# State space stage: TensorE's work pinned to an order written out by hand

## The chip, the cores and the metric

One core of one Trainium2 chip runs the whole program. The time is the device time of one execution in microseconds (us); of three executions of the kernel before, the median is 1193.76 us (1191.71 to 1194.17). TensorE (PE in the profile) does matrix products and transposes, VectorE (DVE) and ScalarE (ACT) work elementwise, SyncE's queue (SP) issues the DMAs.

## The reference, cut to what matters

Two layers act on 256 latent tokens and 256 context tokens of width 1024. Layer 0 is attention and a feed-forward part; layer 1 is a state space mixer, whose context stream only supplies the states, and a feed-forward part on the latent stream. The change lies in the state space mixer:

```python
z, xbc, dt = jnp.split(u @ w_in, [SSM_D_INNER, SSM_D_INNER + SSM_CONV_DIM], axis=-1)
xbc = jax.nn.silu(depthwise_conv(xbc, conv_w, conv_b))
xs, bm, cm = jnp.split(xbc, ...)                      # x: 32 heads of 64; B and C: 4 groups of 128
dt = jax.nn.softplus(dt + dt_bias)                    # two directions x 32 heads
# per direction: a = dt * a_neg, a_cs = cumsum(a)
states = einsum(B, exp(a_cs[-1] - a_cs), x * dt)      # of the context
y_diag = einsum((C B^T) * exp(segsum(a)), x * dt)     # latent, inside the sequence
y_off  = einsum(C, states, exp(a_cs))                 # latent, from the context's states
y = (y_f + y_b + x * d_skip) * silu(z)
y = y * rsqrt(mean(square(y)) + eps) * norm_g         # mean over each of 4 groups of 512 channels
y_lat = y @ w_out
```

## The kernel before, in words

All projections run on weights that come as 1 MB blocks (`raw`) through SP's queue; each 128-wide weight tile is split into a high part (`wh`, ScalarE, L61) and a low part (`wl`, VectorE, L62), and a product (`gemm`, L75) is 24 matmuls: eight k steps of high times high, high times low, low times high. Up to two tiles are split ahead (`next_w`); four split tiles and two `raw` blocks have room.

The state space stage (`layer1`, L976) works on channels times tokens, in four groups of 512 channels. It takes, in the program's order:

- six `z` products (256 columns, L825), then `dt_chain` (L770): the product `dt` (its own weight block `wdt`, split at L777 and L778), some 25 VectorE instructions (L787 to L817, among them a reciprocal and a scan) with three ScalarE exponentials, two small DMAs to `dq` in DRAM, and four transposes (L821, L822) whose result `sT` holds per-token factors.
- `ssm_in(g)` for each group g: products B (512 columns) and C (256), four x tiles (512 columns: latent and context) and, from group 1 on, the rest of the z tiles (two in group 1, four in groups 2 and 3). Each of B, C and x goes through `conv` (L747): ScalarE reads the bank, four VectorE instructions (L758) add the taps, ScalarE takes tanh, one or two VectorE instructions (L763) give the result. Each x tile is then transposed to tokens (L868, L869: four transposes) and scaled by `sT` into `xt` (ScalarE, eight instructions, L875) and `xw` (VectorE, L878). After x tile 0 come the products of C and B (`cb`, L885) and B's transposes (`bt`, L894). Last come the context's states `S` (L905).
- `ssd(g)` for each group: for each of four tiles, A and E are loaded from `dq` (L924, L925), ScalarE and VectorE make the masked factors W and the scaled C in E (L931 to L935), TensorE makes y (L947: 12 products of fp32, 24 matmul records, on half the array's columns, 128x64), VectorE finishes y (L949, L951), ScalarE squares it, and TensorE sums the squares (`rms`, L954, on a quarter of the columns, 128x32). Then `rstd` (L206) makes the group's root: a copy, two small products (`t`), square root and reciprocal, two products that spread it (`b`), and y is normalised and split (L963 to L965).

`weave` (L968) alternates a step of `ssd(g-1)` with a step of `ssm_in(g)`; after group 3 it alternates `ssd(3)` with the output products `so`. That is only the order in which the program is traced. A planner then lays out each engine's instructions: it goes through all of them in time, by its own estimates of durations, and gives each engine the earliest-traced instruction that is ready; so a ready product overtakes a transpose that waits. On the chip each engine goes through its list in order. PSUM has eight banks: four `mm` (products), three `aux` (transposes, `cb`, y, S, the root, and `rms` over a whole `ssd`), one `md`.

Of the kernel before, what the change touches and what calls it, by code (L numbers as in the profile page):

```python
# [8 lines left out]
F32 = mybir.dt.float32  # L9
# [27 lines left out]
NZ = 6  # L37


class Net:  # L40
# [23 lines left out]
    def next_w(self, ahead=2, whole=False):  # L64
# [8 lines left out]
        return wh.rearrange("p (k c) -> p k c", c=128), wl.rearrange("p (k c) -> p k c", c=128)  # L73

    def gemm(self, ps, w, ah, al, c0, c1, ks=range(8)):  # L75
        mm = self.nc.tensor.matmul
# [86 lines left out]
    def run(self, gen):  # L163
        for _ in gen:
            pass

# [38 lines left out]

    def rstd(self, ps, nm, scale, eps):  # L206
# [12 lines left out]
        for i in range(2):  # L219
            c = slice(128 * i, 128 * i + 128)  # L220
            nc.vector.tensor_scalar(d[:, c], self.ident, r[:, i:i + 1], 32.0 * 1024, op0=ALU.mult, op1=ALU.mult)
            nc.tensor.matmul(b[:, c], self.avg, d[:, c], start=True, stop=True)
        return b[:, :256]

    def ln_joint(self, s, nm, mps, X):
        nc = self.nc
        mu = self.spread(mps, nm + "m")
        vps = self.bank("aux", f"{nm}v")
        for q in range(4):
            xs = X[:, 2 * q:2 * q + 2, :]  # L230
            nc.vector.tensor_tensor(xs, xs, mu.unsqueeze(1).broadcast_to([128, 2, 256]), op=ALU.subtract)
            sq = self.t2.tile([128, 2, 256], F32, tag="t2", name=f"{nm}q")
            nc.scalar.activation(sq, xs, AF.Square)
            self.colsum(vps, sq, range(2 * q, 2 * q + 2))
        return self.rstd(vps, nm + "w", 1.0, self.eps)

# [533 lines left out]
    def dt_chain(self, uh, ul):  # L770
        nc, tc = self.nc, self.tc
        mm = nc.tensor.matmul
# [7 lines left out]
        ps = self.bank("mm", "dt")[:64, :]  # L780
# [36 lines left out]
        st(R[64:128], R[64:128], 0.125, dt[64:128], op0=ALU.mult, op1=ALU.mult)  # L817
        pt = self.bank("aux", "dtt", (128, 384))
        for i in range(2):
            c = slice(128 * i, 128 * i + 128)  # L820
            nc.tensor.transpose(pt[:, 192 * i:192 * i + 128], R[:, c], self.ident)  # L821
            nc.tensor.transpose(pt[:, 192 * i + 128:192 * i + 192], dt[0:64, c], self.ident[:64, :64])  # L822
        nc.scalar.copy(self.sT, pt.rearrange("p (i h) -> p i h", i=2))

# [11 lines left out]
    def ssm_in(self, g, uh, ul):  # L836

        nc = self.nc
        mm = nc.tensor.matmul
        sp = self.sp  # L840
# [16 lines left out]
        Bt = sp.tile([128, 2, 128], F32, tag="Bt", name=f"Bt{g}")  # L857
        for j in range(4):
            w = self.next_w()
            ps = self.bank("mm", f"x{g}{j}")  # L860
            self.gemm(ps, w, uh, ul, 0, 512)
            xl = self.xl()
            xc = sp.tile([128, 256], F32, tag="xc", name=f"xc{g}{j}")
            G["xl"].append(xl)
            self.conv(ps, 4 * g + j, 2, [xl, xc])
            pt = self.bank("aux", f"xt{g}{j}")
            for i in range(2):
                nc.tensor.transpose(pt[:, 128 * i:128 * i + 128], xl[:, 128 * i:128 * i + 128], self.ident)  # L868
                nc.tensor.transpose(pt[:, 256 + 128 * i:384 + 128 * i], xc[:, 128 * i:128 * i + 128], self.ident)  # L869
            for d in range(2):  # L870
                o = 128 + 32 * d + 8 * g + 2 * j
                for i in range(2):
# [8 lines left out]
                    self.sT[:, :, o:o + 2].unsqueeze(3).broadcast_to([128, 2, 2, 64]), op=ALU.mult)  # L881
            if j == 0:
                pb = self.bank("aux", f"cb{g}")
                for i in range(2):
                    mm(pb[:, 256 * i:256 * i + 256], B[:, 128 * i:128 * i + 128], C, start=True, stop=True)  # L885
                cf = G["cb0"] = sp.tile([128, 384], F32, tag="cf", name=f"cf{g}")
                cb = G["cb1"] = sp.tile([128, 384], F32, tag="cb", name=f"cb{g}")
                nc.vector.tensor_mul(cf[:, 0:256], pb[:, 0:256], self.tri[:, 0:256])
                nc.vector.tensor_mul(cf[:, 256:384], pb[:, 384:512], self.tri[:, 0:128])
                nc.vector.tensor_mul(cb[:, 0:128], pb[:, 0:128], self.tri[:, 256:384])  # L890
                nc.vector.tensor_mul(cb[:, 128:384], pb[:, 256:512], self.tri[:, 128:384])
                pb = self.bank("aux", f"bt{g}", (128, 256))
                for i in range(2):
                    nc.tensor.transpose(pb[:, 128 * i:128 * i + 128], B[:, 256 + 128 * i:384 + 128 * i], self.ident)  # L894
                nc.scalar.copy(Bt, pb.rearrange("p (i n) -> p i n", i=2))
            yield
        if g:
            for j in range(max(4 * g, NZ), 4 * g + 4):
                self.z_tile(j, uh, ul)
                yield  # L900
        G["S"] = []
# [9 lines left out]
    def ssd(self, g, yh, yl):  # L911
        nc = self.nc
        sp = self.sp
        mm = nc.tensor.matmul
        G = self.G[g]
        ys = []
        rps = self.bank("aux", f"rms{g}")
        for j in range(4):
            M, Cs = [], []
            for d in range(2):  # L920
# [16 lines left out]
                Cs.append(E)  # L937
            yield
            ps = self.bank("aux", f"y{g}{j}")[:, :256]
# [13 lines left out]
            nc.scalar.activation(sq, y, AF.Square)  # L953
            mm(rps[32 * j:32 * j + 32, :256], self.ones, sq, start=True, stop=True)  # L954
            ys.append(y)
            yield

        rs = self.rstd(rps, f"rms{g}", 2.0, self.eps4)
        for j in range(4):
# [16 lines left out]
    def layer1(self):  # L976
# [12 lines left out]
        with tc.tile_pool(name="dq", bufs=1, space=DRAM) as dqp:  # L989
            dq = dqp.tile([2, 64, 256], F32, name="dq")  # L990
            self.dq = dq
            with tc.tile_pool(name="sp", bufs=2) as sp:
                self.sp = _Multi(tc, sp, dict(cy=2, ct=1, B=1, C=2, xt0=2, xt1=2, xw0=1, xw1=1, Bt=1, xc=1,
                                              cf=2, cb=2, S0=1, S1=1, A=2, E=2, W=2))
                for j in range(NZ):
                    self.z_tile(j, uh, ul)
                self.dt_chain(uh, ul)
                self.run(self.ssm_in(0, uh, ul))
                for g in range(1, 4):
                    self.weave(self.ssd(g - 1, yh, yl), self.ssm_in(g, uh, ul))  # L1000
                acc = [[self.bank("mm", f"so{i}{h}") for h in range(2)] for i in range(2)]
# [172 lines left out]
```

## Time and profile before

| | |
|---|---|
| median of three executions | 1193.76 us |
| the profiled execution | 1194.7 us |
| its span, first to last instruction | 1192.9 us |
| PE busy | 1140.3 us, 96% |
| DVE busy | 839.5 us, 70% |
| ACT busy | 604.3 us, 51% |
| mean granted TensorE clock | 0.984 of full |

A matmul's duration in the profile contains filling and draining that overlap its neighbours, so the distance from one start to the next is what it costs. The state space stage runs from about 660 us (first z product) to about 978 us (`so`, with the last group's root inside).

### The profile page before, as it was taken

What the parts mean: (1) busy time and instruction counts of PE and PEld (TensorE: products, weight loads), DVE (VectorE), ACT (ScalarE), POOL (GpSimd) and SP (SyncE); (2) the same over time, 40 slices, a digit from 0 to 9 for tenths busy, and PEclk for the clock granted to TensorE, in tenths of its full rate; (3) what the DMA queues carried; (4) which work ended last, traced back from release to release, by engine and by line L of the source; (5) the groups of instructions that cost most, each with busy time, mean ns of one, the idle gap of its engine ahead of it and who ended that gap; (6) DMA issues with size and microseconds to landing.
All of it is one profiled execution on the core that took longest, in us unless ns stands there. A gap on an engine that the chain in (4) does not pass through costs nothing.

```text
span 1192.9 us, 18539 instructions
## 1 busy us (share of the span) xinstructions
PE 1140.3 (96%) x6976; PEld 917.5 (77%) x6976; DVE 839.5 (70%) x1701; ACT 604.3 (51%) x1382; POOL 48.1 (4%) x79
## 2 busy tenths in 40 slices
PE   5999999998999999999999999999999996999996
PEld 4766666887987878887898777777777575898895
DVE  4498677677967677763434879889898769565566
ACT  4376566325532322321422737687868857454551
POOL 1200000003100000000000310000000000000000
PEclk8999999999999999999999989999999998999999
DMA  8834322342445466762222124443545572555551
GB/s 323 305 106 156 128 85 94 91 157 72 159 160 182 157 226 207 249 215 92 85 71 87 64 107 128 131 153 129 189 142 155 186 242 83 200 177 182 202 181 71
DMA packets 41433, 182.79 MB, mean 153 GB/s; under 512 B 4608, under 2 KB 5248, under 8 KB 28288
## 3 DMA queue, kind: packets, MB, share of 16 engines
q1 hardware_dynamic: 41056, 181.36, 45.1%
q8 instruction: 55, 0.90, 0.3%
q10 hardware_dynamic: 288, 0.26, 0.1%
q14 instruction: 34, 0.28, 0.1%
HBM read 180.41 MB, written 1.18 MB: 152 GB/s over the span
## 4 chain that ended last, share of the span: by engine, by line
PE 79%; DVE 8%; DMA 5%; ACT 5%; issue 1%; DVEq 0%; SPq 0%; ACTq 0%
PE f0a L79 5%; PE f0a L80 5%; PE f0a L81 5%; PE f0b L79 5%; PE f0b L81 5%; PE f0b L80 5%; PE y L947 3%; PE o L508 2%; PE f L265 2%; PE f L264 2%; PE f L263 2%; PE f1a L81 2%; PE f1a L79 2%; PE f1a L80 2%; DMA raw<-in_wall 2%; PE x L81 2%
## 5 line engine op out<-in xcount | busy, mean ns | idle before, releaser
L61 ACT CAST wh<-raw 128x512 fp32r<-128x512 f32 x404 | 237.6, 619 | 400.5 <-PE f0b L80 126.3
L62 DVE TENSOR_TENSOR wl<-raw,wh 128x512 fp32r<-128x512 f32 x404 | 268.4, 686 | 129.3 <-ACT wh L61 128.4
L79 PE MATMUL f0b<-f0fh,wh 128*128 128x512 f32 (+1 forms) x320 | 113.8, 356 | 0.0
L79 PE MATMUL f0a<-u1h,wh 128*128 128x512 f32 (+1 forms) x320 | 112.2, 353 | 1.5 <-ACT u1h L183 1.5
L81 PE MATMUL f0b<-f0fh,wl 128*128 128x512 f32 (+1 forms) x320 | 111.9, 350 | 0.0
L80 PE MATMUL f0a<-u1l,wh 128*128 128x512 f32 (+1 forms) x320 | 111.4, 350 | 0.0
L81 PE MATMUL f0a<-u1h,wl 128*128 128x512 f32 (+1 forms) x320 | 111.4, 349 | 0.0
L80 PE MATMUL f0b<-f0fl,wh 128*128 128x512 f32 (+1 forms) x320 | 111.1, 347 | 0.1
L142 DVE SCALAR_TENSOR_TENSOR ma<-wm,cs,ma 128x1024 f32<-128x1024 f32 x70 | 88.7, 1280 | 17.8 <-DMA wm<-in_w_mod 17.7
L79 PEld LDWEIGHTS f0a<-u1h,wh 128*128 128x128 f32 x320 | 61.1, 192 | 11.8 <-ACT u1h L183 2.3
L81 PEld LDWEIGHTS f0b<-f0fh,wl 128*128 128x128 f32 x320 | 60.1, 188 | 10.4 <-issue 2.1
L79 PEld LDWEIGHTS f0b<-f0fh,wh 128*128 128x128 f32 x320 | 60.1, 188 | 10.4 <-issue 2.6
L80 PEld LDWEIGHTS f0b<-f0fl,wh 128*128 128x128 f32 x320 | 60.2, 188 | 9.7 <-issue 1.4
L81 PEld LDWEIGHTS f0a<-u1h,wl 128*128 128x128 f32 x320 | 61.2, 191 | 8.0 <-issue 0.4
L80 PEld LDWEIGHTS f0a<-u1l,wh 128*128 128x128 f32 x320 | 61.0, 191 | 7.7 <-issue 0.4
L79 PE MATMUL f1a<-u4h,wh 128*128 128x256 f32 x224 | 63.5, 284 | 0.0
L81 PE MATMUL f1a<-u4h,wl 128*128 128x256 f32 x224 | 63.5, 283 | 0.0
L80 PE MATMUL f1a<-u4l,wh 128*128 128x256 f32 x224 | 63.4, 283 | 0.0
L79 PE MATMUL x<-u2h,wh 128*128 128x512 f32 x128 | 51.5, 402 | 2.2 <-DVE cy L758 2.2
L931 ACT ACTIVATE W<-A,sT 128x128 f32<-128x128 f32 (+1 forms) x128 | 50.0, 458 | 3.8 <-PE y L947 2.5
L351 DVE SCALAR_TENSOR_TENSOR X<-f0b,mT,X 128x256 f32<-128x256 f32 x48 | 21.0, 478 | 44.0 <-PE f0b L81 44.0
L81 PE MATMUL x<-u2h,wl 128*128 128x512 f32 x128 | 51.3, 402 | 0.3 <-DVE wl L62 0.3
(439 smaller groups left out, 2747.3 us busy)
## 6 DMA issues: line engine op xcount, KB each, us to landing
raw<-in_wall SPq DMA_DIRECT2D x102, 1024.0 KB, 5.0
wm<-in_w_mod SPq DMA_DIRECT2D x96, 512.0 KB, 4.3
A<-dq SPq DMA_DIRECT2D x32, 256.0 KB, 4.7
E<-dq SPq DMA_DIRECT2D x32, 256.0 KB, 5.0
X<-in_xT SPq DMA_DIRECT2D x8, 256.0 KB, 8.1
gate<-in_rows SPq DMA_DIRECT2D x2, 512.0 KB, 12.9
out_dram<-Xt SPq DMA_DIRECT2D x4, 256.0 KB, 2.0
mixg<-in_rows SPq DMA_DIRECT2D x1, 512.0 KB, 6.1
```

The source lines that it names most:

```text
L61: nc.scalar.copy(h, src[:, c])
L62: nc.vector.tensor_sub(l, src[:, c], h.bitcast(F32))
L79: mm(ps, wh[:, k, :], ah[k][:, c0:c1], start=(k == 0), stop=False)
L80: mm(ps, wh[:, k, :], al[k][:, c0:c1], start=False, stop=False)
L81: mm(ps, wl[:, k, :], ah[k][:, c0:c1], start=False, stop=(k == 7))
L142: nc.vector.scalar_tensor_tensor(t, wm, c, t, op0=ALU.mult, op1=ALU.add)
L263: mm(ps, lh(i), wh[:, c], start=(k == 0), stop=False)
L264: mm(ps, ll(i), wh[:, c], start=False, stop=False)
L265: mm(ps, lh(i), wl[:, c], start=False, stop=last)
L508: nc.tensor.matmul(po[64 * a:64 * a + 64, :], self.V[:, kt, g * 64:g * 64 + 64], PT[a][:, i * n:i * n + n], start=(i == 0), stop=(i == len ...
L931: nc.scalar.activation(W[:, h, o:o + l1 - l0], A[:, h, l0:l1], AF.Relu, scale=-1.0, bias=self.sT[:, st, r + h:r + h + 1])
L947: mm(ps[64 * a:64 * a + 64, l0:l1], lh[:, hc:hc + 64], mv, start=(n == 0), stop=(n == 5))
```

## The change

Every matmul and transpose that the stage traces, from group 0's B up to group 3's states, is pinned: it may not be issued before the TensorE instruction traced before it. Not pinned are the six first z products, `dt`'s product (only what follows is queued behind its last matmul), and `ssd(3)` with `so`. The other engines are still laid out by the planner. The traced order itself is new:

- an x tile's transposes (`tokens`) stand after the next x product; the last tile's after two z products (in group 0: after group 1's B);
- `bt` and `cb` (`bc`) stand after x tile 1's product, `bt` first;
- `dt`'s four transposes and the copy to `sT` (`finish`) stand after group 0's x tile 0;
- the states of a group stand after the next group's C (group 0) or B (groups 1 and 2); group 3's after all its z products;
- in `ssd`, a tile's factors (`prep`) are traced right after the y before it, a tile's `rms` sum just before the next y, and the root's two halves at steps of their own;
- `rms` takes the bank `md`, so that `aux` keeps its three banks;
- `rstd` makes both scaled identities before both spreading products (in layer 0's norms too).

No instruction is added or taken away on any engine, and each shape is as before.

```diff
+    def pin(self, on):
+        if on:
+            self.mm = lambda *a, **k: self.tc.keep_in_program_order(self.nc.tensor.matmul(*a, **k))
+            self.tr = lambda *a, **k: self.tc.keep_in_program_order(self.nc.tensor.transpose(*a, **k))
+        else:
+            self.mm, self.tr = self.nc.tensor.matmul, self.nc.tensor.transpose
...
         for i in range(2):
-            nc.tensor.matmul(t[:, i:i + 1], sm[:, 128 * i:128 * i + 128], self.avg[:, 0:1], start=True, stop=True)
+            self.mm(t[:, i:i + 1], sm[:, 128 * i:128 * i + 128], self.avg[:, 0:1], start=True, stop=True)
+        yield
...
+        def finish():
+            pt = self.bank("aux", "dtt", (128, 384))
+            for i in range(2):
...
+                self.tr(pt[:, 192 * i:192 * i + 128], R[:, c], self.ident)
+                self.tr(pt[:, 192 * i + 128:192 * i + 192], dt[0:64, c], self.ident[:64, :64])
+            nc.scalar.copy(self.sT, pt.rearrange("p (i h) -> p i h", i=2))
+        return finish
...
+        left = None
+        for j in range(4):
...
+            self.conv(ps, 4 * g + j, 2, [xl, xc])
+            if j == 1:
+                bc()
+            if left is not None:
+                tokens(*left)
+            left = (j, xl, xc)
             yield
+        zs = range(max(4 * g, NZ), 4 * g + 4) if g else ()
+        for i, j in enumerate(zs):
+            self.z_tile(j, uh, ul)
+            if i == 1:
+                tokens(*left)
+                left = None
+            yield
+        if left is not None:
+            yield
+            tokens(*left)
+        yield
         G["S"] = []
...
-        rps = self.bank("aux", f"rms{g}")
+        rps = self.bank("md", f"rms{g}")
...
+        M, Cs = prep(0)
+        yield
+        for j in range(4):
+            if j > 0:
+                square(j - 1)
             ps = self.bank("aux", f"y{g}{j}")[:, :256]
...
+            if j < 3:
+                M, Cs = prep(j + 1)
             yield
+        square(3)
+        yield
+        rs = yield from self.rstd_steps(rps, f"rms{g}", 2.0, self.eps4)
...
-                self.dt_chain(uh, ul)
-                self.run(self.ssm_in(0, uh, ul))
+                dt = self.dt_chain(uh, ul)
+                self.pin(True)
+                old = self.ssm_in(0, uh, ul)
+                for n in range(7):
+                    next(old)
+                    if n == 2:
+                        dt()
+                rest = iter(())
                 for g in range(1, 4):
-                    self.weave(self.ssd(g - 1, yh, yl), self.ssm_in(g, uh, ul))
+                    b = self.ssd(g - 1, yh, yl)
+                    next(b)
+                    new = self.ssm_in(g, uh, ul)
+                    for n in range(8 if g == 1 else 11):
+                        next(new)
+                        if n == 0:
+                            self.run(rest)
+                        if n < (2 if g == 1 else 1):
+                            next(old)
+                        else:
+                            next(b, None)
+                    if g == 1:
+                        next(new)
+                    old, rest = new, b
+                next(old)
+                self.run(rest)
+                self.pin(False)
```

Read out, TensorE's order from `dt` on is: dt, B, C and x0 of group 0, dt's transposes, x1, `bt`, `cb`, tokens 0, x2, tokens 1, x3, tokens 2; group 1's B, tokens 3 of group 0, C, group 0's states, x0, y0, x1, `bt`, `cb`, tokens 0, sum 0, y1, x2, tokens 1, sum 1, y2, x3, tokens 2, sum 2, y3, z, sum 3, z, tokens 3, root's first half. In groups 2 and 3: B, the last group's root (second half, group 2 only), its states, C, y0, x0, sum 0, y1, x1, `bt`, `cb`, tokens 0, sum 1, y2, x2, tokens 1, sum 2, y3, x3, tokens 2, sum 3, z, root's first half, z, tokens 3, root's second half, z, z.

## Rows read from the trace of the kernel before

**Rows 1.** Stretches of the stage: bounds, length, PE, PEld, DVE, ACT, POOL busy (instructions); clock; DMA.
```profile
684.00:704.00 20.00, 16.47 (x72) 12.30 (x73) 13.22 (x29) 7.80 (x16) 6.33 (x6) 0.83 0.30 108
704.00:738.00 34.00, 33.94 (x169) 28.04 (x169) 32.54 (x69) 21.08 (x53) 0.00 (x0) 1.00 0.41 126
738.00:752.00 14.00, 11.16 (x42) 5.89 (x43) 11.95 (x22) 8.80 (x25) 0.00 (x0) 0.76 0.33 115
752.00:926.00 174.00, 173.25 (x1031) 131.34 (x1028) 152.45 (x293) 137.69 (x345) 0.00 (x0) 1.00 0.47 150
```
**Rows 2.** PE in order of time around 684: start, duration, instruction [idle before <-releaser].
```profile
683.54 0.28 PE L80 MATMUL z<-u2l,wh 128*128 128x256 f32 x1
683.66 0.28 PE L81 MATMUL z<-u2h,wl 128*128 128x256 f32 x1
...
684.94 0.40 PE L80 MATMUL dt<-u2l,wdth 128*64 128x512 f32 x1
688.21 0.80 PE L79 MATMUL B<-u2h,wh 128*128 128x512 f32 x1 [2.87 <-DVE z L833]
```
**Rows 3.** VectorE in order of time, dt's weights and its chain.
```profile
691.15 0.68 DVE L778 TENSOR_TENSOR wdtl<-wdt,wdth 128x512 fp32r<-128x512 f32 x1
...
699.86 0.97 DVE L787 TENSOR_SCALAR X<-dt,vecs 64x256 f32<-64x256 f32 x2 [2.02 <-PE dt L81]
...
721.28 0.42 DVE L817 SCALAR_TENSOR_TENSOR X<-X 64x256 f32<-64x256 f32 x1
```
**Rows 4.** PE in order of time, end of dt's product and dt's transposes.
```profile
699.13 0.39 PE L80 MATMUL dt<-u2l,wdth 128*64 128x512 f32 x1
699.35 0.39 PE L81 MATMUL dt<-u2h,wdtl 128*64 128x512 f32 x1
...
721.88 0.28 PE L821 MATMUL dtt<-con,X 128*128 128x128 f32 x1
```
**Rows 5.** PE in order of time, from group 1's x0 through group 0's states to y.
```profile
740.81 0.61 PE L79 MATMUL x<-u2h,wh 128*128 128x512 f32 x1 [2.24 <-DVE cy L758]
...
745.55 0.63 PE L79 MATMUL x<-u2h,wh 128*128 128x512 f32 x1
745.98 1.05 PE L905 MATMUL S<-xw,Bt 128*128 128x512 f32 x1
...
750.42 1.52 PE L947 MATMUL y<-W,xt 128*64 128x256 f32 x16
...
752.74 0.50 PE L80 MATMUL x<-u2l,wh 128*128 128x512 f32 x1
```
**Rows 6.** PE in order of time, a lone sum of squares and a y cut in pieces.
```profile
835.22 0.39 PE L80 MATMUL x<-u2l,wh 128*128 128x512 f32 x1
835.54 0.62 PE L954 MATMUL rms<-ysq,ones 128*32 128x256 f32 x2
836.09 0.50 PE L81 MATMUL x<-u2h,wl 128*128 128x512 f32 x1
...
841.14 0.65 PE L947 MATMUL y<-W,xt 128*64 128x256 f32 x2
841.72 0.33 PE L869 MATMUL xt<-con,xc 128*128 128x128 f32 x1
```
**Rows 7.** ScalarE in order of time: where two x tiles' conv begins.
```profile
758.03 0.77 ACT L752 ACTIVATE cy<-x,vecs 128x512 f32<-128x512 f32 x1
...
778.93 0.78 ACT L752 ACTIVATE cy<-x,vecs 128x512 f32<-128x512 f32 x1 [0.36 <-PE x L81]
```
**Rows 8.** VectorE in order of time: where these two end; factors after a y.
```profile
765.44 0.42 DVE L763 SCALAR_TENSOR_TENSOR xc<-ct,cy 128x256 f32<-128x256 f32 x1
...
789.24 0.42 DVE L763 SCALAR_TENSOR_TENSOR xc<-ct,cy 128x256 f32<-128x256 f32 x1
...
832.89 0.48 DVE L949 SCALAR_TENSOR_TENSOR X<-X,dsk,y 128x256 f32<-128x256 f32 x1
...
837.36 0.94 DVE L934 TENSOR_TENSOR W<-W,cb 128x768 f32<-128x768 f32 x1
```

More of the change, by code (lines that the diff above doesn't have):

```diff
@@ L163, in run @@
     def run(self, gen):
-        for _ in gen:
-            pass
+        while True:
+            try:
+                next(gen)
+            except StopIteration as e:
+                return e.value
     def affine(self, name, gv, bv, streams, scale, shift):
@@ L204, in spread, with rstd_steps @@
         return b[:, :256]
-    def rstd(self, ps, nm, scale, eps):
+    def rstd_steps(self, ps, nm, scale, eps):
         nc = self.nc
@@ L221, in rstd @@
             nc.vector.tensor_scalar(d[:, c], self.ident, r[:, i:i + 1], 32.0 * 1024, op0=ALU.mult, op1=ALU.mult)
-            nc.tensor.matmul(b[:, c], self.avg, d[:, c], start=True, stop=True)
+        for i in range(2):
+            c = slice(128 * i, 128 * i + 128)
+            self.mm(b[:, c], self.avg, d[:, c], start=True, stop=True)
         return b[:, :256]
@@ L234, in ln_joint @@
             self.colsum(vps, sq, range(2 * q, 2 * q + 2))
-        return self.rstd(vps, nm + "w", 1.0, self.eps)
+        return self.run(self.rstd_steps(vps, nm + "w", 1.0, self.eps))
     def ln(self, s, nm, bank, aff, uh, ul, X):
@@ L817, in dt_chain @@
         st(R[64:128], R[64:128], 0.125, dt[64:128], op0=ALU.mult, op1=ALU.mult)
[L818 to L823, printed above, removed]
+        def finish():
+            pt = self.bank("aux", "dtt", (128, 384))
+            for i in range(2):
+                c = slice(128 * i, 128 * i + 128)
+                self.tr(pt[:, 192 * i:192 * i + 128], R[:, c], self.ident)
+                self.tr(pt[:, 192 * i + 128:192 * i + 192], dt[0:64, c], self.ident[:64, :64])
+            nc.scalar.copy(self.sT, pt.rearrange("p (i h) -> p i h", i=2))
+        return finish
     def z_tile(self, j, uh, ul):
@@ L838, in ssm_in @@
         nc = self.nc
-        mm = nc.tensor.matmul
+        mm, tr = self.mm, self.tr
         sp = self.sp
@@ L881, in ssm_in @@
                     self.sT[:, :, o:o + 2].unsqueeze(3).broadcast_to([128, 2, 2, 64]), op=ALU.mult)
[L882 to L895, printed above, removed]
-            yield
[L897 to L900, printed above, removed]
+        left = None
+        for j in range(4):
+            w = self.next_w()
+            ps = self.bank("mm", f"x{g}{j}")
+            self.gemm(ps, w, uh, ul, 0, 512)
+            xl = self.xl()
+            xc = sp.tile([128, 256], F32, tag="xc", name=f"xc{g}{j}")
+            G["xl"].append(xl)
+            self.conv(ps, 4 * g + j, 2, [xl, xc])
[4 more added lines that the diff above has]
+            left = (j, xl, xc)
+            yield
+        zs = range(max(4 * g, NZ), 4 * g + 4) if g else ()
[9 more added lines that the diff above has]
+        yield
         G["S"] = []
@@ L913, in ssd, with prep @@
         sp = self.sp
-        mm = nc.tensor.matmul
+        mm = self.mm
         G = self.G[g]
-        ys = []
-        rps = self.bank("aux", f"rms{g}")
-        for j in range(4):
+        ys, sqs = [], []
+        rps = self.bank("md", f"rms{g}")
+        def prep(j):
             M, Cs = [], []
@@ L937, in ssd, with square @@
                 Cs.append(E)
-            yield
+            return M, Cs
+        def square(j):
+            mm(rps[32 * j:32 * j + 32, :256], self.ones, sqs[j], start=True, stop=True)
+        M, Cs = prep(0)
[3 more added lines that the diff above has]
+                square(j - 1)
             ps = self.bank("aux", f"y{g}{j}")[:, :256]
@@ L953, in ssd @@
             nc.scalar.activation(sq, y, AF.Square)
-            mm(rps[32 * j:32 * j + 32, :256], self.ones, sq, start=True, stop=True)
+            sqs.append(sq)
             ys.append(y)
+            if j < 3:
+                M, Cs = prep(j + 1)
             yield
-        rs = self.rstd(rps, f"rms{g}", 2.0, self.eps4)
+        square(3)
+        yield
+        rs = yield from self.rstd_steps(rps, f"rms{g}", 2.0, self.eps4)
         for j in range(4):
```

30 lines of the change are left out of this document (19 added, 11 removed).

## The prediction

> **What bounds the kernel now.** I read the stage's stretches first [rows 1]. From 752 to 926 PE is busy 173.25 of 174 us at full clock: TensorE is never idle there, and a new order can save only what changing between kinds of work costs. VectorE is busy 152.45 us of the same 174, ScalarE 137.69, so neither has much to give. The stage's beginning is different. From 684 to 704 PE is busy 16.47 of 20 us, and a mean clock of 0.83 means that 2 x 0.17 x 20 = 6.8 us of it ran at 1.2 instead of 2.4 GHz; from 738 to 752 it is busy 11.16 of 14 us with 2 x 0.24 x 14 = 6.7 us at 1.2 GHz. Between the two, VectorE is busy 32.54 of 34 us. The second thing to read is therefore PE in order of time around 684: `z` ends, two matmuls of `dt` start, and nothing follows until B at 688.21 [rows 2]. Third, VectorE in order of time [rows 3]: `wdtl`, which dt's third matmul reads, is made at 691.15 to 691.83; dt's chain starts at 699.86 and ends with L817 at 721.70; dt's transposes follow at 721.88 [rows 4].
>
> The change leaves every engine as much to compute. So I count, in us, what TensorE loses or saves: first in the start of the stage, up to the end of group 0's states, then in the rest.
>
> **Unit costs.** A 512-column matmul costs 0.22 to 0.23 from start to start [rows 4], so a product of 24 is 5.45; at 1.2 GHz it is 0.43 [rows 5]. A 256-column one costs 0.12 [rows 2], so C or z is 2.9. A whole y is 2.32 [rows 5]. Group 0's states took 4.44 at the lower clock in part [rows 5]; eight at 0.43, fp32 in two passes, give 3.4 at the full one (estimate: twice 0.22 each).
>
> **Start, part 1: dt's product.** Before, B filled the wait for `wdtl`: 17 of its 24 matmuls ran between 688.21 and 694.5, dt's other 22 after them. Now B is queued behind dt's last matmul, and TensorE stands from 685.2 to 691.9. Nothing traced before dt's split changes, so I keep `wdtl` where it is. As both idle stretches came with some 6.8 us at 1.2 GHz, part of it while TensorE still stood [rows 1, 2], I take 4.8 us of dt at 0.43 (11 matmuls) and 11 at 0.23: 7.3, so dt ends near 699.2, as before (699.58 [rows 4]). VectorE's chain starts no later. But B is all still to do: it ends at 704.7, C at 707.6, x0 at 713.1. Before, x0 ended 3.9 earlier.
>
> **Start, part 2: dt's transposes.** They were free before: TensorE did x0, x1, x2 and part of x3 and B while VectorE needed 21.8 us for the chain [rows 3]. Now x1 and all behind it on TensorE wait for them, and VectorE's conv of x1 waits for x1. When is the chain done? Between the first and the last row of it [rows 3] its 26 instructions take some 10.6 us of the 21.8; the other 11.2 are conv of B, C and x0 (16 instructions) and five weight splits, put between. These now come later (B's conv 5.5 us after dt instead of 1.6), so fewer lie inside: B 3.3, C 1.95, some 2.5 of splits, instead of 11.2. Bounds: alone, with about 2 for the exponentials on ScalarE and the handing over, it would end at 712.5, before x0 does, and no wait is left; with all that lay inside before, at 721.7. I take 718, since the planner alternated the two kinds as soon as both were there. TensorE stands 4.9 us (713.1 to 718.0), and the clock then costs 2.5 to 3.4 more (of some 6.8 us at half, 5.0 to 6.8 with TensorE at work); I take 3.
>
> **Start, the sum.** From 718.0: dt's transposes 0.9, x1 to x3 16.35, group 1's B 5.45, C 2.9, `cb` with `bt` 1.1, four tiles' transposes 1.8, clock 3, a wait of 1 for x2's conv (its transposes come only 5.9 behind x2): states start at 750.5, end at 753.9. Before they end at 750.42 with nine matmuls of the next x done [rows 5], worth 2.0: 748.4. So **+5.5**, between -2.4 (no wait for the chain, no lower clock) and +9.2 (chain as before).
>
> **The rest: changes between kinds of work.** A lone sum costs more than its two matmuls: x to sum 0.32, sum to x 0.55, and the x behind it lasts 0.50 instead of 0.39 [rows 6]; 0.32 + 0.55 + 0.11 less 0.23 and less 2 x 0.12 for the two is 0.5. A y piece of two records takes 0.58 [rows 6] where a record of a whole y takes 2.32/24 = 0.1; with the 0.1 on either side, each piece costs about 0.4. From 752 to 926 the records hold, of the kinds of which rows 6 show one each, 12 sums standing alone and 19 pieces of y (the planner cut some y in two or three around another tile's transposes): 12 x 0.5 + 19 x 0.4 = 13.6. After, three y and three sums stand alone and nine sums stand right before a y, with one way in and one way out saved (0.2): 3 x 0.4 + 3 x 0.5 + 9 x 0.7 = 9.0. Saving **-4.6**, between -2.8 (a sum before a y costs as much as two apart) and -6.4 (the change from sum to y is free). No row has a sum right before a y; I take the middle, as their shapes differ (128x32, 128x64) but the full array isn't visited between.
> In these rows a matmul next to one of another tile shape starts late. The Trainium skill, TensorEngine Tiling (Array Packing), section Key Properties, says that changing the tiling mode, not just the tile, drains TensorE. By it the step from sum to y is a drain too, which speaks against the end of -6.4 and leaves -2.8 to -4.6.
>
> **The rest: waits taken away.** TensorE's idle time from 752 to 926 is 0.75 us [rows 1]. With three `aux` banks free for turning, as `rms` sits in `md`, I let it go: **-0.8**; more there isn't.
>
> **The rest: waits added.** Now an x tile's transposes wait at a fixed place, and behind them on TensorE stand sum, y and the next product, on which VectorE's and ScalarE's conv wait in turn. Conv took 758.03 to 765.86 = 7.8 us at best and 778.93 to 789.66 = 10.7 at worst [rows 7, 8]. The room from an x tile's end to its transposes, from the unit costs, is 9.4, 9.9, 8.8 and 7.2 for tiles 0 to 3 in groups 2 and 3, and 8.9, 9.9, 8.8, 9.7 in group 1. At 7.8 the shortfalls sum to 1.2; at 10.7 to 20.9; at the mean, 9.3, to 6.3. A wait at one tile gives the next ones time, so I take **+4**. A y has 6.2 us or more behind the last one; its second factor W came at 838.3, 5.4 behind the start of that y's eviction at 832.89 [rows 8], and is read only a third into y: covered, by the product between; without that cover it would cost about 1 each. Loads of A and E go out right behind a y as before, the same 64, a little ahead of `raw` in SP's queue; splitting `rstd`'s loop moves two matmuls by 0.3 us behind VectorE; the unpinned `so` still covers the last root (52 us of work around it). Nothing for these.
>
> **Sum.** 5.5 - 4.6 - 0.8 + 4 = +4.1. The profiled execution took 1194.7 (span 1192.9); it lies 0.9 above the median of 1193.76. So 1198.8 by the profile, 1197.9 as a median; I say 1198.
>
> **Rivals.**
> *Faster: dt's chain is in time.* If the planner lets the chain run ahead of conv on VectorE, R is ready when x0 ends, at 713; below about 714 nothing is lost. For it: the chain's instructions are traced before every conv, and by 705.7 only they and x1's splits are ready. Against: before, every second slot went to conv. It removes 4.9 + 3 of the 1198: 1190.
> *Clearly slower: the fixed queue turns each late conv into idle TensorE.* VectorE is busy 88% from 752 to 926 [rows 1], and where x and y alternate it has some 9 us of work for each 8.9 of TensorE. If conv takes its worst 10.7 throughout, waits are 20.9; from about 9.5 on they outweigh the savings. Two thirds of it, 13 instead of 4: 1207.
> *No change: the planner's order was near the written one.* Sums joined for -6.4, waits 1.2, the rest as forecast: 5.5 - 6.4 - 0.8 + 1.2 = -0.5, that is 1193.3.
>
> **How the numbers follow.** About 0.2% (2.4 us) is what a measurement here tells from no change. Forecast 0.45 (its own range 1193 to 1202: 0.16 within 0.2%, 0.29 slower); chain in time 0.27 (0.22 faster, 0.05 same); fixed queue 0.17 (slower); no change 0.11 (0.07 same, 0.04 faster). Faster 0.26, same 0.28, slower 0.46. The bounds end at 5.5 - 7.9 - 6.4 - 0.8 + 1.2 = -8.4 and at 9.2 - 2.8 + 20.9 = +27; I leave the outer ends out: 1187 to 1208.
>
> **What would show it.** Right: PE idle of some 6.5 us before dt's third matmul and of about 5 before `dtt`, each with a lower clock; states of group 0 ending near 754; from there sums directly before y, no cut y, a few waits of up to 2 us on L763. Wrong: `dtt` directly behind x0 (first rival); waits on L763 or L934 at nearly every tile (second); `wdtl` much earlier than 691, which would shift the whole start.

## The result, and the profile after

The changed kernel takes 1200.53 us (median of four, 1198.86 to 1202.08); the kernel before, run beside it, 1192.74 (1191.45 to 1194.17). The ratio is 1.0063, 95% interval 1.0047 to 1.0080: slower by 7.8 us, where 1198 was forecast. The profiled execution, the slowest of the four, took 1202.08, its span 1200.3, its mean clock 0.981.

First the stage's stretches, in the columns of [rows 1]:

```profile
684.00:704.00 20.00, 13.48 (x54) 9.42 (x55) 13.51 (x29) 5.64 (x12) 5.61 (x4) 0.83 0.40 142
704.00:738.00 34.00, 28.65 (x128) 22.78 (x128) 30.43 (x64) 19.52 (x48) 0.00 (x0) 0.90 0.43 122
738.00:752.00 14.00, 12.52 (x67) 9.74 (x66) 12.47 (x24) 9.84 (x27) 0.00 (x0) 1.00 0.22 75
752.00:926.00 174.00, 170.12 (x1028) 132.20 (x1027) 154.43 (x298) 141.81 (x351) 0.00 (x0) 0.98 0.47 146
```

TensorE now stands for 3 us more in the first stretch and for over 5 in the second, where it was hardly ever idle (0.06 us), and even between 752 and 926 it is idle for 3.9 us, at a mean clock of 0.98 instead of 1.00. What it stood for says the list of waits of PE, 660 to 990 us (total, times, longest):

```profile
PE dt L89 <- DVE wdtl L794: 6.6, 1, 6.6
PE dtt L79 <- DVE X L833: 5.3, 1, 5.3
PE xt L79 <- DVE X L779: 4.8, 3, 1.6
...
```

The two large ones in order of time on PE: dt's product, which B filled before [rows 2], and dt's transposes, which came late at no price before [rows 4]. The last two rows are the end of group 0's states [rows 5]:

```profile
683.28 0.45 PE L87 MATMUL dt<-u2h,wdth 128*64 128x512 f32 x1 [0.71 <-ACT wdth L793]
683.56 0.40 PE L88 MATMUL dt<-u2l,wdth 128*64 128x512 f32 x1
690.52 0.69 PE L89 MATMUL dt<-u2h,wdtl 128*64 128x512 f32 x1 [6.56 <-DVE wdtl L794]
...
697.68 0.39 PE L78 MATMUL B<-u2h,wh 128*128 128x512 f32 x1
...
711.23 0.39 PE L78 MATMUL x<-u2h,wl 128*128 128x512 f32 x1
716.96 1.45 PE L79 MATMUL dtt<-con,X 128*128 128x128 f32 x4 [5.34 <-DVE X L833]
...
750.21 3.59 PE L78 MATMUL S<-xw,Bt 128*128 128x512 f32 x8
753.24 0.79 PE L78 MATMUL x<-u2h,wh 128*128 128x512 f32 x1
```

VectorE's side of it [rows 3]: `wdtl` as late as before, but for the 1.4 by which this execution came to the stage earlier, and the chain's first and last instruction, 18.9 us apart instead of 21.8, with conv and weight splits still taking every second slot between:

```profile
689.78 0.68 DVE L794 TENSOR_TENSOR wdtl<-wdt,wdth 128x512 fp32r<-128x512 f32 x1
...
697.95 0.97 DVE L803 TENSOR_SCALAR X<-dt,vecs 64x256 f32<-64x256 f32 x2 [1.39 <-PE dt L89]
...
716.39 0.42 DVE L833 SCALAR_TENSOR_TENSOR X<-X 64x256 f32<-64x256 f32 x1
```

**Where the time went.** The profiles are cut at four points of PE: dt's first matmul, the end of group 0's states, the end of group 3's, and `xr` behind the stage. To compare equal work, product matmuls done ahead of a cut are taken off at 0.2265 each (5.44 for 24): nine of x before the first cut and twelve of `so` before the second in the kernel before, none after (of x 15 in e5 and e9, 9 in e10, 6 in e11; of `so` 3 in e9, 36 in e10). Before, 750.42 - 684.66 - 9 x 0.2265 = 63.7; after, 753.24 - 683.28 = 70.0. The four leave out what lies ahead of dt. Two edits touch it: e3's, and the new order in `rstd`, which layer 0's norms use too. Of the latter no loss shows: the first z product begins at 656.6 to 660.8 in the three kernels without it, at 656.0 to 659.6 in those with it, and from there to dt it is 24.4 us in all but e3. So dt's beginning, between 680.4 and 685.2 without e3 (683.28 is 1.4 earlier than 684.66), scatters with what lies ahead of the stage. The same reading of every experiment, whose medians stand against the kernel before, run beside it:

| kernel | start | rest | to `xr` | to end | sum against before | measured |
|---|---|---|---|---|---|---|
| before | 63.7 | 177.4 | 52.3 | 214.9 | | |
| changed | 70.0 | 178.1 | 53.0 | 215.9 | +8.8 | +7.8 |
| e1 dt's transposes after x1 | 70.1 | 176.9 | 52.9 | 214.9 | +6.5 | +8.5 |
| e1p the same, tanh first | 69.4 | 178.3 | 52.9 | 214.8 | +7.1 | +5.1 |
| e2 held behind B and C | 73.2 | 178.1 | 53.4 | 216.0 | +12.4 | +11.9 |
| e3 dt's weights early | | 178.0 | 52.7 | 215.0 | | +6.8 |
| e4 root later | 70.6 | 175.9 | 53.0 | 215.7 | +6.9 | +7.8 |
| e4b tokens 3 later | 70.7 | 171.6 | 53.3 | 214.8 | +2.1 | +2.1 |
| e6 held from group 1 | 66.6 | 178.5 | 53.0 | 214.8 | +4.7 | +2.6 |
| e8 held behind the states, tokens 3 later | 64.5 | 172.2 | 53.5 | 214.8 | -3.2 | -2.6 |
| e5 nothing held | 62.9 | 173.0 | 53.6 | 215.1 | -3.7 | -3.6 |
| e9 nothing held, tokens 3 later | 62.3 | 173.6 | 51.8 | 215.7 | -4.8 | -4.6 |
| e10 before, sums late | 62.3 | 179.5 | 52.1 | 215.3 | +1.0 | +1.7 |
| e11 before, tokens late | 63.5 | 176.9 | 51.0 | 215.7 | -1.1 | -0.7 |

So the loss is +6.2 in the start, +0.7 in the rest and +0.8 up to `xr`. The column to the end, 214.8 to 216.0, goes with no edit and is taken for scatter; with its 1.1 left out, +7.7 meets the measured +7.8. Over all twelve kernels sum and measurement differ by up to 2.1, so a difference of that size between two rows need not be one between their medians.

**The rest in rows.** A sum now stands right before a y (PE in order of time; compare the lone sum and the cut y of [rows 6]):

```profile
837.04 0.62 PE L78 MATMUL rms<-ysq,ones 128*32 128x256 f32 x2
837.59 1.52 PE L78 MATMUL y<-W,xt 128*64 128x256 f32 x16
...
839.90 0.50 PE L78 MATMUL x<-u2h,wh 128*128 128x512 f32 x1
```

The sum takes 0.55 to the y behind it, the same as to an x product: the step from a quarter of the columns to half of them isn't free, but one way out and one way in are saved, and y is whole, 2.31. What uses that up is tile 3's transposes. ScalarE's list in order of time, group 2:

```profile
850.13 1.28 ACT L228 ACT_TABLE_LOAD   x1
851.43 0.26 ACT L228 ACTIVATE rms1r<-rms1t,eps 128x2 f32<-128x2 f32 x1
851.59 0.61 ACT L61 CAST wh<-raw 128x512 fp32r<-128x512 f32 x1
852.22 1.28 ACT L776 ACT_TABLE_LOAD   x1
853.51 0.63 ACT L776 ACTIVATE ct<-cy 128x512 f32<-128x512 f32 x1
```

The root's square root (L228) needs another function table than tanh (L776). Two loads, the root and a cast come between conv's taps and its tanh; the half of x3's conv that the first transpose reads ends at 854.6, and TensorE has stood for it. PE's row, and a stretch of windows from there:

```profile
854.65 0.33 PE L79 MATMUL xt<-con,X 128*128 128x128 f32 x1 [1.64 <-DVE X L779]
```
```profile
854.60:858.00 3.40, 3.34 (x17) 3.15 (x18) 3.40 (x9) 3.26 (x12) 0.00 (x0) 0.62 0.31 130
858.00:864.00 6.00, 6.00 (x45) 5.86 (x45) 4.16 (x10) 3.35 (x11) 0.00 (x0) 0.93 0.10 15
```

After the wait the clock is down: 0.38 x 3.4 + 0.07 x 6.0 = 1.7 us of work lost, as much as the wait itself. Group 3 shows the same: loads at 915.3 and 917.4, a wait of 1.64 at tile 3's transposes at 919.82, and 0.57 as the clock's mean over the 3.4 us behind it. Not every wait does: behind the 1.48 us at 740.70 the clock stayed at 1.00 (the stretch from 738 to 752 above).

### The profile page after: what moved, and what is told of

It is laid out like the page before. It is cut to its first block, busy times and chain, and to the rows that moved or that the text cites. A ratio compares the mean times of both kernels' runs of the same rounds, so it can differ in the third digit from the quotient of the medians.

```text
span 1200.3 us, 18543 instructions
## 1 busy us (share of the span) xinstructions
PE 1138.1 (95%) x6976; PEld 918.6 (77%) x6976; DVE 840.3 (70%) x1701; ACT 605.6 (50%) x1382; POOL 48.0 (4%) x79
## 4 chain that ended last, share of the span: by engine, by line
PE 83%; DVE 8%; ACT 4%; DMA 3%; issue 1%; DVEq 0%; SPq 0%; ACTq 0%
PE x L78 7%; PE f0a L87 5%; PE f0a L88 5%; PE f0a L89 5%; PE f0b L87 5%; PE f0b L89 5%; PE f0b L88 5%; PE o L523 2%; PE f L280 2%; PE f L279 2%; PE f L278 2%; PE f1a L89 2%; PE f1a L87 2%; PE f1a L88 2%; PE y L78 2%; PE B L78 2%
## 5 line engine op out<-in xcount | busy, mean ns | idle before, releaser
L150 DVE SCALAR_TENSOR_TENSOR ma<-wm,cs,ma 128x1024 f32<-128x1024 f32 x70 | 88.7, 1281 | 21.0 <-DMA wm<-in_w_mod 20.9
L87 PE MATMUL f1a<-u4h,wh 128*128 128x256 f32 x224 | 63.5, 284 | 0.0
L78 PE MATMUL x<-u2l,wh 128*128 128x512 f32 x128 | 50.7, 396 | 0.0
```

Source lines behind the costliest of these rows:

```text
L78: self.mm = lambda *a, **k: self.tc.keep_in_program_order(self.nc.tensor.matmul(*a, **k))
L150: nc.vector.scalar_tensor_tensor(t, wm, c, t, op0=ALU.mult, op1=ALU.add)
```

## Experiments

The theory I went in with: the waits that the held order makes cost what they last, plus the clock; taking one away gives its time back. The rival: they are one chain, and a wait that goes comes back as another.

### The start: one wait at a time

**e1**, dt's transposes one product later:
```diff
             if j == 1:
+                if dt is not None:
+                    dt()
                 bc()
...
-                old = self.ssm_in(0, uh, ul)
+                old = self.ssm_in(0, uh, ul, dt)
                 for n in range(7):
                     next(old)
-                    if n == 2:
-                        dt()
```


> dt's four transposes stand one product later, after group 0's x1 instead of x0. Theory (TensorE's wait for the chain is itself the loss): x1's 5.45 us cover the 5.3 us wait for R, and the lower clock behind it goes too: 5.3 + 2.5 = 7.8 us less, 1192.7. Rival (VectorE, busy 30.4 of 34 us from 704 to 738, bounds the start): the wait comes back in front of the tokens of x1 to x3, and no more than the 3.6 us that VectorE has idle there come off: about 1197.

Measured 1200.61, ratio 1.0072 (1.0057 to 1.0088). The wait at `dtt` is gone and another, of 6.3 us, stands at tokens 0. The waits of PE in this kernel:

```profile
PE xt L79 <- DVE X L779: 11.4, 4, 6.3
PE dt L89 <- DVE wdtl L794: 6.5, 1, 6.5
...
```

The theory fell: group 0's states end at 753.27, against 753.24. The rival's 1197 was missed too. ScalarE in order of time names who is late:

```profile
720.50 1.49 ACT L971 ACTIVATE W<-A,sT 128x256 f32<-128x256 f32 x4 [1.23 <-DMA A<-dq]
724.00 0.40 ACT L971 ACTIVATE W<-A,sT 128x128 f32<-128x128 f32 x1 [2.01 <-DMA A<-dq]
724.30 0.61 ACT L776 ACTIVATE ct<-cy 128x512 f32<-128x512 f32 x1
```

x0's tanh stands in ScalarE's list behind a W for the first y, which waits for A, a load from `dq` that dt's chain stored.

**e1p**, the same with these W activations kept behind everything traced before them, so that tanh goes first:
```diff
+                        w = nc.scalar.activation(W[:, h, o:o + l1 - l0], A[:, h, l0:l1], AF.Relu, scale=-1.0,
+                                                 bias=self.sT[:, st, r + h:r + h + 1])
+                        if g == 0 and j == 0:
+                            self.tc.keep_in_program_order(w)
```


> As the run with dt's transposes one product later (1200.61 us), and group 0's first W activations on ScalarE stay behind everything that the text has before them, so that tanh of x0 to x2 no longer stands behind a W that waits for A's load. Theory (the wait at the transposes of tokens 0 was ScalarE's queue order, a second blocker and not the chain): tokens 0 follow x2 without a wait, the 6.3 us and part of its lower clock go, group 0's states end 5 to 8 us earlier than 753.2, time 1193 to 1195. Rival (VectorE and ScalarE have that much work between dt and the states in any order): the wait moves on, to tokens 1, to B's transposes or to W before the first y; states end within 2 us of 753; 1199 to 1201.

Measured 1197.61, ratio 1.0039 (1.0023 to 1.0055), between the two. The wait at tokens 0 is down from 6.3 to 3.6, and a new one of 1.3 stands before group 0's states; by the profile the start is only 0.6 shorter than e1's:

```profile
PE xt L79 <- DVE X L779: 7.5, 4, 3.6
...
PE S L78 <- DVE xw L907: 1.3, 1, 1.3
...
```

The ten executions lie between 1194.02 and 1200.33, and the profiled one took 1200.09; what the median has gained beyond that 0.6 can't be read from it.

**e3**, dt's weight load and split traced ahead of the z products (a new `dt_weights()`, called before them), so that `wdtl` is there in time:
```diff
+                self.dt_weights()
                 for j in range(NZ):
                     self.z_tile(j, uh, ul)
```


> dt's weights are loaded and split before the first z product instead of after the sixth. Theory (the start is one chain: dt's product, VectorE's chain, dt's transposes): dt's product no longer waits 6.6 us for wdtl, only for the last parts of its input at about 686.5, and ends near 688 instead of 697.7; VectorE still has z and weight splits until 690.5, so the chain ends some 7 to 8 us earlier, at about 709, and the time falls by 7 to 8 us, 1193. The wait before dt's transposes then stays or grows, since x0 comes earlier as well. Rival (each wait counts by itself): 6.6 us of waiting and some 2.5 of lower clock go and the second wait stays at 5.3: 1191.5.

Measured 1198.92, ratio 1.0041 (1.0024 to 1.0058); the seven executions lie between 1194.12 and 1199.99, and the profiled one is the slowest. The wait for `wdtl` is gone, but dt's first matmul now stands 5.3 us, by the row for VectorE's part of an earlier z product, and the planner, which is free there, put most of the last z product inside dt's. dt's transposes wait as they did:

```profile
PE dtt L79 <- DVE X L837: 5.5, 1, 5.5
PE dt L87 <- DVE z L856: 5.3, 1, 5.3
...
```

With z inside dt's product the first cut doesn't part equal work here. Counted from the first z product, the way to the end of group 0's states is 88.1 us before (after the same nine matmuls), 94.4 in the changed kernel and 93.0 in e3: 1.4 of the 6.6 were gained.

**e2**, held only from behind group 0's B and C (`pin(True)` after the second step), so that B fills dt's wait as before:
```diff
...
-                self.pin(True)
...
                 for n in range(7):
                     next(old)
+                    if n == 1:
+                        self.pin(True)
```


> The changed kernel, pinned only from behind group 0's B and C, so that B may fill dt's wait for wdtl again; dt's transposes stay pinned behind x0. Theory (the start is bounded by VectorE's chain and what follows it, since dt itself ends no earlier): x0 ends some 5 us earlier, dt's transposes then wait some 9 to 10 us instead of 5.3, and the states end within 1.5 us of 753.2: 1199 to 1201. Rival (each wait counts by itself): the 6.6 us and its lower clock go and nothing comes back, 1194 to 1197.

Measured 1204.41, ratio 1.0091 (1.0060 to 1.0121): 3.9 us worse than the changed kernel. B does fill the wait, x0 ends near 705.2, and TensorE stands longer at the next place:

```profile
705.01 0.39 PE L78 MATMUL x<-u2h,wl 128*128 128x512 f32 x1
717.57 1.45 PE L79 MATMUL dtt<-con,X 128*128 128x128 f32 x4 [12.17 <-DVE X L833]
```

From dt's first matmul to `dtt` it is 37.2 us here, 37.2 before and 33.7 in the changed kernel. The earlier B, C and x0 are done, the earlier VectorE does their conv between the chain's instructions. The theory's direction held; the price was larger than expected.

**e6**, group 0 not held at all (`pin(True)` where group 1 begins):
```diff
...
-                self.pin(True)
...
+                self.pin(True)
                 rest = iter(())
                 for g in range(1, 4):
```


> Group 0's own steps (B to tokens 2, dt's transposes) are traced in the new order but not pinned; pinning begins with group 1's B. Theory (the start costs 6.2 us because of the two waits that pinning makes there, and the rest costs 1 to 3): the planner again fills both waits, group 0's states end at about 748.5 in the profile, and the time falls by about 6 us to 1194 to 1195, near the kernel before. Rival (the loss comes from the pinned groups 1 to 3 and the wait only moves there): above 1198.

Measured 1194.70, ratio 1.0023 (1.0008 to 1.0038): the fall of some 6 us came. Both waits are gone, but group 1's B is held behind group 0's tokens 2, and these come late (the first row):

```profile
PE xt L860 <- DVE X L779: 6.3, 1, 6.3
PE xt L79 <- DVE X L779: 3.6, 2, 1.9
PE B L87 <- DVE z L852: 2.9, 1, 2.9
...
```

So within the start the rival is right: the five waits that e1, e2, e3 and e6 take away all came back at other places, in e6 at a price 3.4 us lower (66.6 for 70.0), in e3 at one 1.4 lower. From dt's product through the chain, the `dq` loads and the conv, one thing follows from another, and only products that TensorE may take out of order fill what is left.

### Tile 3's transposes

**e4**, the root's halves one step later in groups 2 and 3, behind the transposes:
```diff
-                        else:
+                        elif g == 1 or n != 6:
                             next(b, None)
```


> In groups 2 and 3 the root's first half stands after tokens 3 instead of one z product before them, its second half one z later. Theory (the tokens of x tile 3 wait because ScalarE runs the root's Sqrt with two table loads of 1.28 us before that tile's tanh): both waits of 1.6 us go, and the lower clock behind each (3.4 us at half, some 1.7 us): 6.6 us less, 1194. Rival (conv is late because VectorE is full): both waits stay at about 1.6 us, time unchanged at 1200.5.

Measured 1199.92, ratio 1.0067 (1.0052 to 1.0082). Group 3's wait went and came back at the root; group 2's stayed, as tanh there stood behind a weight cast that waited for its block. The rest is 2.2 shorter by the table, the median 0.6. That gain is the clock's, not the waits': TensorE is idle for 4.5 us from 752 to 926, more than the changed kernel's 3.9, but at a mean clock of 1.00 instead of 0.98. The stretch, the waits of PE, and ScalarE in order of time in group 2:

```profile
752.00:926.00 174.00, 169.50 (x1038) 130.59 (x1037) 155.41 (x300) 143.38 (x355) 0.00 (x0) 1.00 0.48 150
```
```profile
...
PE xt L79 <- DVE X L779: 2.7, 2, 1.5
PE rms2b L78 <- DVE rms2d L234: 1.8, 1, 1.8
...
PE rms1b L78 <- DVE rms1d L234: 0.9, 1, 0.9
```
```profile
853.04 1.14 ACT L61 CAST wh<-raw 128x512 fp32r<-128x512 f32 x2 [1.36 <-DMA raw<-in_wall]
854.08 0.62 ACT L776 ACTIVATE ct<-cy 128x512 f32<-128x512 f32 x1
```

**e4b**, these transposes after the third of z products instead of the second:
```diff
-            if i == 1:
+            if i == len(zs) // 2:
                 tokens(*left)
```


> As the changed kernel, but in groups 2 and 3 the transposes of tile 3 come after the third of the five z products instead of after the second. Theory (the two waits of 1.6 us at tokens 3 and the lower clock behind each, some 1.7 us each, come only from ScalarE's conv of x3 being late behind the root's table loads): both waits and both lower-clock stretches go, -4 to -6.6 us, 1194 to 1196.5 against 1200.5. Rival (weights for the z products or room in the turning banks is as late): the wait comes back at z or at the sum, less than 2 us are gained, 1198.5 to 1200.5.

Measured 1194.66, ratio 1.0011 (0.9996 to 1.0026): 5.9 us less than the changed kernel. The theory holds: no wait for conv is left in PE's list from 754.5 to 926, and the stretch runs at full clock.

```profile
PE rms L78 <- ACT ysq L1000: 0.6, 1, 0.6
PE rms2b L78 <- DVE rms2d L234: 0.2, 1, 0.2
PE rms1b L78 <- DVE rms1d L234: 0.2, 1, 0.2
```
```profile
752.00:926.00 174.00, 173.11 (x1057) 133.18 (x1056) 158.32 (x308) 145.21 (x360) 0.00 (x0) 1.00 0.47 148
```

The rest falls from 178.1 to 171.6: two waits of 1.6 with 1.7 of clock each make 6.6.

### What the held order itself is worth

**e5**, the changed kernel's text with nothing held:
```diff
-                self.pin(True)
+                self.pin(False)
```


> The changed kernel's text order, late transposes and places, but the planner may order TensorE again (nothing pinned). Theory (the loss is the pinned queue's: waits at wdtl 6.6, at dt's transposes 5.3, at tokens 3 and at the root, with the clock after them): B fills the wait for wdtl, x products fill the chain's, S of group 0 ends near 748, as before, and the planner cuts y and sums apart again as before, so that the joint switches' saving of some 4 us goes too: 1191 to 1195. Rival (the new places in the text cost by themselves: dt's transposes, states, so and sums later): 1198 to 1201 with the pin off as well.

Measured 1188.96, ratio 0.9965 (0.9952 to 0.9979): faster than before, and 11.6 us faster than the changed kernel. My expectation had the waits right and the sums wrong: the time came out below its range. The planner doesn't part the sums from y again: seven of the twelve in groups 0 to 2 stand right before a y (none in the kernel before), and y has 16 pieces in the rest, where it had 20. The stretch in which `dtt` was waited for, now all but full, and a sum before the first piece of a y, on PE in order of time:

```profile
704.00:738.00 34.00, 33.03 (x164) 27.08 (x162) 32.72 (x70) 21.13 (x54) 0.00 (x0) 1.00 0.40 125
```
```profile
811.85 0.62 PE L979 MATMUL rms<-ysq,ones 128*32 128x256 f32 x2
812.40 0.87 PE L994 MATMUL y<-W,xt 128*64 128x256 f32 x8
```

The start is as short as before's (62.9, 63.7), the rest 4.4 shorter.

**e9**, e5 with e4b's edit:
```diff
-                self.pin(True)
+                self.pin(False)
...
-            if i == 1:
+            if i == len(zs) // 2:
```


> The changed kernel's text with nothing pinned, and tokens 3 after the third z in groups 2 and 3. Theory (a place in the text matters to a held TensorE only; a free one puts the transposes where they are ready): as without it, 1188.96, within 1.5 us. Rival (the written place steers the planner as well, as the sums' place seems to): 2 to 4 us less.

Measured 1188.14, ratio 0.9964 (0.9950 to 0.9978): the same as e5 within its runs. A place that mattered to a held TensorE doesn't to a free one. Its median is the lowest of the study, though not told apart from e5's.

**e8**, everything up to group 0's states left free, held from there, with e4b's edit:
```diff
-            if i == 1:
+            if i == len(zs) // 2:
...
-                self.pin(True)
...
                         if n < (2 if g == 1 else 1):
                             next(old)
+                            if n == 1:
+                                self.pin(True)
```


> Everything up to group 0's states is left to the planner; TensorE is held in written order only from behind them, and in groups 2 and 3 the transposes of tile 3 come after the third z. Theory (the held order costs in the start, some 6.5 us, and at tokens 3, 5.9 us, and nowhere else, and these two add): states as in the run with nothing pinned or up to 2 us later, because nothing behind them can fill their waits; the rest as in the run with tokens 3 late (171.6 us): 1187 us (1185.5 to 1189), below both kernels. Rival (the planner's freedom in the rest is worth something too, or waits at group 1's tokens come back behind the states): 1190 to 1193.

Measured 1190.16, ratio 0.9979 (0.9965 to 0.9993). By the table both parts are as the theory has them: the start 1.6 longer than e5's, the rest 172.2 against e4b's 171.6. The median is at the rival's lower end; adding the parts from e5 (1188.96 + 1.6 - 0.8 = 1189.8) I should have expected 1190. The profiled execution, 1187.86, is the fastest of twelve (up to 1194.49). So by the profiles held and free TensorE do equally well in the rest, once no wait is written into it.

**e10 and e11**, the kernel before with one part of the new text alone: the sums late, or the transposes late.
```diff
...
             yield
+            if j > 0:
+                square(j - 1)
             ps = self.bank("aux", f"y{g}{j}")[:, :256]
...
```


> The kernel before with one part of the change alone: the sum over a tile's squares is written right before the next tile's y instead of behind its own, nothing pinned. Theory (the joint changes between kinds of work come from the place of the sums in the text, and need no pin): eight or nine of the twelve sums stand beside a y, 0.4 to 0.5 us each, 1188 to 1190 us against 1192.5. Rival (a free planner puts the sums where it likes, and the unpinned changed kernel gained by its late transposes): within 1 us of before, 1191.5 to 1193.

```diff
...
+            if left is not None:
+                tokens(*left)
+            left = (j, xl, xc)
             yield
+        zs = range(max(4 * g, NZ), 4 * g + 4) if g else ()
+        for i, j in enumerate(zs):
+            self.z_tile(j, uh, ul)
+            if i == 1:
+                tokens(*left)
...
```


> The kernel before with another part alone: each x tile's transposes are written one product late (tile 3's behind the second z), nothing pinned. Theory (they cut less into y, but most of the saving is the sums'): -0.5 to -2 us, 1190.5 to 1192. Rival (the late transposes are what the unpinned changed kernel gained by): -3 to -4 us, 1188.5 to 1189.5.

e10: 1194.47, ratio 1.0020 (1.0011 to 1.0028), a little slower than before. e11: 1192.09, ratio 0.9999 (0.9988 to 1.0010). e10's theory of 2.5 to 4.5 us less fell, and with it e11's view that most of the saving is the sums'; e11's own -0.5 to -2 is met at its small end (-0.7, within the noise). Both rivals, by which the late transposes make e5 fast, fell with e11: neither part does it alone. e10's PE rows show that a sum's place in the text isn't its place on TensorE:

```profile
826.15 0.62 PE L920 MATMUL rms<-ysq,ones 128*32 128x256 f32 x2
...
828.29 1.52 PE L953 MATMUL y<-W,xt 128*64 128x256 f32 x16
```

The sum is taken when it is ready, and y is not yet; none of e10's twelve stands beside a y. The change also traces a tile's factors W one step earlier, right behind the y before. That fits, since y is then ready when the sum is, but it wasn't tried alone; nor were `rms` in `md` and the new sequence of products. Which of them turns the 4.4 us stays open.

## Why the prediction was right, point by point

- *Start, +5.5; measured +6.2.* Part 1 is as forecast: TensorE stood 6.6 us for `wdtl`, at half clock behind it to 694.8, and dt ended no later. Forecast for the end of B, C and x0: 704.7, 707.6, 713.1; with the 1.4 by which this execution came to the stage earlier that is 703.3, 706.2, 711.7, and the rows have 703.1, 706.0, 711.5. Part 2 too: I took 718 for the chain, 716.6 with the shift; it is 716.96, and the wait 5.3 for 4.9. That the planner alternates chain and conv was the step that decided, against the first rival. The states came 0.7 later than I summed; 0.5 of that is the wait for x2's conv at tokens 2, 1.5 where I had allowed 1.
- *Changes between kinds of work, -4.6, and waits taken away, -0.8; measured about -5.8 together.* e4b's rest against before's, 171.6 and 177.4, is this sum without the waits at tile 3. The order came out as counted (nine sums right before a y, three sums and three y alone). But the -0.8 didn't come: e4b's TensorE is idle for 0.9 us from 752 to 926 (174 less 173.11), as it was before for 0.75. So the changes alone gave about -5.8, near the free end of -6.4, and sizing them from sums and y left something out: other products are cut less too (B in the rest stands in 2 pieces in e4b and in 9 before, x in 12 and 19). What a sum before a y saves by itself is therefore not shown. The step from sum to y isn't free: its two 256-column records take 0.55 to the y behind them, where such a record is 0.12 among its like [rows 2]. The Trainium skill, TensorEngine Tiling (Array Packing), section Key Properties, says that a change of the tiling mode, not just of the tile, drains TensorE; that 0.55 agrees, but the bound of -4.6 that I drew from it was passed.
- *Waits added, +4; measured +6.5* (178.1 for e4b's 171.6), inside the bounds of 1.2 and 20.9, but mis-sized: I had spread it over the tiles by conv's length. It all sits at tile 3 of groups 2 and 3, the place that the room of 7.2 named as the tightest. (The 6.3 that the prediction gives for conv at 9.3 is 6.1 by its own rooms; +4 was chosen freely below either.) Two things were missing from the term: the root's table loads, which stand in ScalarE's list just there, and the clock, which I counted in the start and not here; in this profile it is half of the price.
- *The way to `xr`, 0; measured +0.8.* All kernels with the new text and a held order have 52.7 to 53.5 there, the kernel before 52.3, and of those with nothing held one has 53.6 and one 51.8. Not taken apart.
- *Sum, +4.1; measured +7.7.* Of the 3.6 that were missing, 2.5 are the waits at tile 3, 0.7 the start, 0.8 the way to `xr`; the changes between kinds of work, with the idle time, give 0.4 back. So the waits and their places were foreseen, and the term that was mis-sized is the waits added. Luck has a small part: the idle time that was to go stayed, and the changes between kinds of work gave 1.2 more than counted, so that the two together fit. The rivals: not the chain in time (`dtt` waited), not a wait at nearly every tile (three waits for conv in all), not the planner's order again.

The prediction never asked what the new text is worth without the hold. e5 answers: -3.6 for the text, +11.6 for the hold, of which the start has 7.1 and the rest 5.1 by the table.

## What to carry to other kernels

Holding an engine to a written order makes each late input cost its wait, and on TensorE at times a lower clock behind it as well; where a free order already keeps the engine busy, write the good order in the text and leave the list free, or hold only stretches whose inputs are known to be in time. Before removing a wait, look for what is late next in the same chain; in the start each one moved on, at tile 3 they went for good (e4b). For each fixed place, read the other engines' lists there, table loads included, not only the length of the work that it waits for.

## What the runs showed of the hardware

- The clock can fall behind waits of only 1.6 us: in the 3.4 us after one it averaged 0.62, that is 2 x 0.38 x 3.4 = 2.6 us at 1.2 GHz. In the 7 us up to that wait PE was busy throughout, at 2.4 GHz (the row below). It doesn't always: waits of 1.48 us in the changed kernel (740.70), of 1.64 in e1 (920.27) and of 1.80 in e4 (924.05) were followed by full clock. So one profile tells what a wait cost in that execution; what decides it stays open here.

```profile
846.00:853.00 7.00, 7.00 (x55) 6.39 (x54) 6.37 (x13) 6.64 (x17) 0.00 (x0) 1.00 0.62 180
```

- A table load took 1.28 us, and the square root behind it began 0.02 later. The Trainium skill, ScalarE: Activation LUTs, section What ACT_TABLE_LOAD costs, gives the same 1283 ns and adds about 1380 ns of draining to each switch. These rows show nothing of the second part. One square root among tanhs costs two loads, 2.6 us of ScalarE's list.
